# A decoder block on one core: the first row tile's scores by one matmul of 256 columns per component, an issue order written out for the passage into the up projection, and one set of transposes held

## The chip, the cores and the metric

The kernel runs on one core of a Trainium2 chip, in one launch. The metric is the device time of an execution in microseconds. Three runs of the kernel before took 675.96, 676.29 and 678.52 us; the median is 676.29.

The engines are named as in the profile: PE is TensorE's matmul, PEld its weight load, DVE is VectorE, ACT is ScalarE, POOL is GpSimd and SP is SyncE, which here only starts DMAs. Each engine works through its own instructions in a fixed order, so an instruction that waits holds back all that stand behind it on its engine.

## What is computed

One layer on 512 tokens of width 1024, all in float32:

```
h = rmsnorm(x, norm_attn_g)
q, k, v, u_pool, u_gate = split(h @ w_in)
for each head (8) and each block of 128 query rows:
    s = (rope(q) * 64**-0.5) @ rope(k).T          # two components of 64 per head
    p = softmax(where(key <= query, s, -inf))
    o = (p[0] - lam * p[1]) @ v
a = rmsnorm(o, subln_g) * (1 - lam_init)
p = causal mean over 2/4/8/16 tokens of u_pool, minus u_pool, @ w_pool, * pool_scale
x = x + (sigmoid(g_A) * a + sigmoid(g_P) * p) @ w_out
x = x + square(relu(rmsnorm(x, norm_mlp_g) @ w_up)) @ w_down
return rmsnorm(x, final_norm_g)
```

## The kernel before

**Precision.** A float32 operand is kept as two parts: `hi`, a copy rounded to the matmul's format (fp32r), and `lo`, the rest. A product is three matmuls: hi by hi, hi by lo and lo by hi. For a weight, ACT makes `hi` (line 112) and DVE the rest (line 113), or a DMA of POOL's that adds.

**The stages.** Up to some 78 us the values of all heads and the rotation tables are made. Then come the eight heads. `qk(h)` projects a head's queries and keys (`proj`, `mm3`, lines 131 to 135: eight k blocks of 512 columns, three matmuls each) and splits them. For scores the parts of one component are stacked in the 128 partitions: `qs` holds the queries' high part in one half and the rest in the other, `ks` and `kz` the matching keys, with zeros in one half of `kz`, so that a score is the sum of two matmuls with the same stationary operand (lines 395 and 396). `attn(h)` takes the query rows in four tiles of 128; tile i has (i + 1) * 128 keys. For each of two components DVE adds the mask and takes the row's extreme (397), ACT makes the exponentials (401), DVE joins the components (406), TensorE transposes blocks of 128 (410), ACT and DVE split the transposed weights (412, 413); last, twelve matmuls with the values make the head's output (418). Score tiles rotate over two PSUM banks (`sbk`), the transposed ones over two others, projections and pooled products over three (`acc`).

Between the heads stand the fillers: per group g of four, `pool(g)` and four gates, each a projection of its own. The multiplication of a gate by the row scale (474) frees its bank.

**The passage.** After the heads comes `w_out` in two halves of 512 columns. The first half accumulates all four row tiles in four banks (`po0`), the second (`po1`) row tile by row tile. `x1_add` adds the residual on DVE (588) and squares on ACT (562); after the second half, `row_scale` and line 624 make the tile's normalized row `h2`, TensorE transposes it in eight blocks (630) into two banks, and ACT and DVE take from these banks the forms in which the up projection wants it. The bank pairs alternate between even and odd tiles, so row tile 2 needs the banks of row tile 0.

The MLP multiplies its blocks of 2 x 2 with seven products in place of eight: A11, A12, A22 are plain blocks of h2 (tiles `gab`), S1 to S4 sums and differences (tiles `gss`, made in `forms_h2`, lines 597 to 604). A form of the first 256 tokens rests on row tiles 0 and 1, A22 and S1 on tiles 2 and 3, and S2, S3 and S4 on all four. For each quarter q of the hidden width, `up(q)` runs the products in the order A11, A12, S1, S2, S3, A22, S4 (q = 0), each in four groups (i, p): eight matmuls with the weights' high part (760, 762) and four with the low part (765), all of 256 columns. `keep` copies a product out of PSUM on ACT, `join` adds one to it on DVE (781). Weights named `wh_ub` and `wl_ub` are plain blocks of `w_up`, `wh_ut` and `wl_ut` sums of blocks. `down(q)` follows.

**What sets the order.** A planner orders each engine's instructions with its own estimate of when they are ready. The kernel adds edges of order to it by `after(later, earlier)`, as here:

```python
if q == 0 and form == A11 and i + p == 2 and k == 0:
    after(m, state["h2T"])
...
if form == A22:
    state["m4"] = m
elif form == S4:
    after(first[-1], state["m4"])
```

The first holds the low-part matmuls of A11's last group behind the last transpose of row tile 3; the second holds the first matmul of S4, and that one alone, behind A22. Between two instructions of one engine such an edge is an order and no wait.

Of the kernel before, what the change touches and what calls it, by code (L numbers as in the profile page):

```python
# [15 lines left out]
ALU = mybir.AluOpType  # L16
# [35 lines left out]
def block_kernel(ctx, tc, xT, x_tok, gains, pos, consts, w_in, w_v, w_pool, w_out, w_up, w_dn, out):  # L52
# [74 lines left out]
    def mm3(acc, hi, lo, rh, rl):  # L127

        for k in range(NK):
            c = slice(k * P, (k + 1) * P)  # L130
            T.matmul(acc, lhsT=hi[:, c], rhs=rh[:, k, :], start=k == 0, stop=False)  # L131
            T.matmul(acc, lhsT=hi[:, c], rhs=rl[k], start=False, stop=False)  # L132
        for k in range(NK):
            c = slice(k * P, (k + 1) * P)
            T.matmul(acc, lhsT=lo[:, c], rhs=rh[:, k, :], start=False, stop=k == NK - 1)  # L135
# [229 lines left out]
    kzs = [cf.tile([P, 2, S], F32R, name=f"kz{i}") for i in range(2)]  # L365
    for kz in kzs:
        G.memset(f(kz)[hi_, 0, :], 0.0)
        G.memset(f(kz)[lo_, 1, :], 0.0)

    def qk(h):  # L370
        qs = tp.tile([P, 2, S], F32R, tag="qs", name=f"qs{h}", bufs=2)
        ks = tp.tile([P, 2, S], F32R, tag="ks", name=f"ks{h}", bufs=2)
        kz = kzs[h % 2]
# [10 lines left out]
        return qs, ks, kz  # L384

    def attn(h, qs, ks, kz):
        wt = wt_all
        for i in range(NT):
# [3 lines left out]
            st = tmp("st", f"st{h}_{i}", (P, 6), bufs=3)  # L392
            for c in range(2):
                s_ = sbk(f"s{h}_{i}_{c}")
                T.matmul(s_[:, :N], lhsT=qs[:, c, qsl], rhs=ks[:, c, :N], start=True, stop=False)
                T.matmul(s_[:, :N], lhsT=qs[:, c, qsl], rhs=kz[:, c, :N], start=False, stop=True)  # L396
                V.tensor_tensor_reduce(  # L397
                    out=pr[:, c, :N], in0=s_[:, :N], in1=mask[:, S - N :], scale=-0.125, scalar=-NEG,
# [10 lines left out]
            for j in range(i + 1):  # L409
                T.transpose(out=t_[:, j * P : j * P + P], in_=pr[:, 0, j * P : j * P + P], identity=ident)  # L410
# [149 lines left out]
    def square(t, n, junk):  # L560

        A.activation(out=junk, in_=x1[:, t, n * 512 : n * 512 + 512], func=AF.Square, accum_out=st[:, t, n : n + 1])
# [16 lines left out]
    def mm_rows(a_, t, k, w, start, stop):  # L579
        hi, lo = w  # L580
        sl, tsl = slice((k % 2) * 512, (k % 2) * 512 + 512), slice(t * P, t * P + P)
        T.matmul(a_, lhsT=mh[:, k, tsl], rhs=hi[:, sl], start=start, stop=False)
        T.matmul(a_, lhsT=mh[:, k, tsl], rhs=lo[:, sl], start=False, stop=False)
        T.matmul(a_, lhsT=ml[:, k, tsl], rhs=hi[:, sl], start=False, stop=stop)

    def x1_add(t, n, a_):
        xs = x1[:, t, n * 512 : n * 512 + 512]
        V.tensor_tensor(out=xs, in0=a_, in1=xs, op=ALU.add)
        square(t, n, R[t][:, 0:2, :].rearrange("p a t -> p (a t)"))
# [22 lines left out]
    for t in range(NT):  # L612
        nc.sync.dma_start(out=x1[:, t, :], in_=x_tok[t])
    for t in range(NT):
        x1_add(t, 0, po[t])
        row_early(t, 0)
    g2b, _ = gain(R[4].rearrange("p b c -> p (b c)"), 0)
    ws = [get_w(w_out[1, kk], f"o1_{kk}", V) for kk in range(4)]
    for t in range(NT):
        a_ = bank(4 + t, f"po1_{t}")  # L620
        for k in range(NK):
            mm_rows(a_, t, k, ws[k // 2], k == 0, k == NK - 1)
# [3 lines left out]
        for b in range(2):  # L626
            pt = bank((t % 2) * 2 + b, f"h2T{t}_{b}")
            for j in range(4):
                k = 4 * b + j
                state["h2T"] = T.transpose(out=pt[:, j * P : j * P + P], in_=h2[:, t % 2, k * P : k * P + P], identity=ident)  # L630
# [115 lines left out]
    def up(q):  # L746
# [3 lines left out]
        def product(form, name, onto=None):  # L750
# [3 lines left out]
            for i in range(2):  # L754
                hi, lo = w[i]
                for p in range(2):
                    a_ = pa[i][:, p * HS : p * HS + HS]
                    for k in range(4):
                        c = slice((p * 4 + k) * P, (p * 4 + k) * P + P)
                        m = T.matmul(a_, lhsT=hi[:, c], rhs=rh[:, k, :], start=p + k == 0 and onto is None, stop=False, skip_group_check=True)  # L760
                        first[-1] = first[-1] or m
                        T.matmul(a_, lhsT=hi[:, c], rhs=rl[:, k, :], start=False, stop=False, skip_group_check=True)  # L762
                    for k in range(4):
                        c = slice((p * 4 + k) * P, (p * 4 + k) * P + P)
                        m = T.matmul(a_, lhsT=lo[:, c], rhs=rh[:, k, :], start=False, stop=k == 3, skip_group_check=True)  # L765
# [28 lines left out]
        def first_block():  # L794
            join(product(A12, "m2"), R[0])
# [198 lines left out]
```

## Time and profile before

| | us |
|---|---|
| median of three runs | 676.29 |
| the profiled execution | 675.88 |
| its span, from first to last instruction | 674.1 |
| PE busy in the span | 664.5 |
| PEld busy | 579.4 |
| DVE busy | 526.4 |
| ACT busy | 461.9 |
| POOL busy | 112.0 |
| TensorE's granted clock, share of full speed | 0.997 |

The profile is that of one execution. A row of a timeline gives the start, the time taken, the engine, the line, the operation, what it writes and reads, the shape and how many were merged; in brackets stands the idle time of the engine ahead of it and what ended that. A matmul's time contains its way through the array, so it overlaps the next one: what a matmul costs a full stream is the distance from its start to the next start. A row of groups gives busy time and mean nanoseconds of one, and behind the bar the idle time before. A row of waits gives who waited for whom, the time in all, how often, and the longest.

### The profile page before, as it was taken

The numbers are of one execution on the slowest core, as the hardware profiler recorded it, in microseconds if no ns is written. First come the engines' busy times: TensorE is split into PE (matmuls) and PEld (weight loads), VectorE is DVE, ScalarE is ACT, GpSimd is POOL, SyncE is SP. The second block draws the span as 40 slices with busy tenths as digits, with TensorE's granted clock in tenths as the row PEclk, the third lists the DMA queues.
The fourth block names the chain that finished last, engine by engine and source line by source line (L and its number), as shares of the span: only waits on it lengthen the run. The fifth ranks groups of instructions, "written<-read, shape, count | busy, mean of one in ns | idle before, by whom it ended". The sixth has DMA issues, their size and how long they took to land.

```text
span 674.1 us, 9988 instructions
## 1 busy us (share of the span) xinstructions
PE 664.5 (99%) x3686; PEld 579.4 (86%) x3686; DVE 526.4 (78%) x882; ACT 461.9 (69%) x741; POOL 112.0 (17%) x130
## 2 busy tenths in 40 slices
PE   9999999999999999999999999999999999999995
PEld 7888888888888888888889988899889998899884
DVE  5955977799979986965478989657994599747995
ACT  7465577978887698883477976367743696356974
POOL 2001110142133212520202020202103021210120
PEclk9999999999999999999999999999999999999998
DMA  8516464435254364574964688775959579494863
GB/s 304 174 60 182 124 150 127 101 95 124 94 133 122 98 159 95 128 197 172 314 186 84 198 176 231 159 204 138 237 187 192 194 155 261 123 215 129 215 125 124
DMA packets 32880, 109.34 MB, mean 162 GB/s; under 512 B 4032, under 2 KB 4928, under 8 KB 32832
## 3 DMA queue, kind: packets, MB, share of 16 engines
q0 software_dynamic: 10656, 38.80, 32.1%
q1 hardware_dynamic: 21744, 69.38, 28.8%
q8 instruction: 29, 0.48, 0.3%
q10 hardware_dynamic: 432, 0.52, 0.2%
q14 instruction: 19, 0.16, 0.1%
HBM read 106.59 MB, written 2.10 MB: 161 GB/s over the span
## 4 chain that ended last, share of the span: by engine, by line
PE 89%; DMA 5%; issue 3%; ACT 2%; DVE 1%; SPq 0%; POOLq 0%
PE dm L839 8%; PE dm L841 7%; PE dm L842 7%; PE um L760 7%; PE um L765 7%; PE um L762 7%; DMA wga_uNone<-w_up 4%; PE v L235 2%; PE o L418 2%; PE ga L132 2%; PE ga L131 2%; PE k L132 2%; PE gp L135 2%; PE gp L132 2%; PE k L131 2%
## 5 line engine op out<-in xcount | busy, mean ns | idle before, releaser
L841 PE MATMUL dm<-wh_dt,z 128*128 128x512 f32 (+1 forms) x128 | 49.5, 387 | 0.0
L842 PE MATMUL dm<-wl_dt,z 128*128 128x512 f32 (+1 forms) x128 | 49.4, 386 | 0.0
L839 PE MATMUL dm<-wh_dt,z 128*128 128x512 f32 (+1 forms) x128 | 49.0, 387 | 0.0
L760 PE MATMUL um<-gss,wh_ut 128*128 128x256 f32 x192 | 48.1, 284 | 0.1
L762 PE MATMUL um<-gss,wh_ut 128*128 128x256 f32 x192 | 48.1, 283 | 0.0
L401 ACT ACTIVATE p<-p,st 128x128 f32<-128x128 f32 (+3 forms) x64 | 35.7, 558 | 14.1 <-DVE st L397 13.8
L857 DVE TENSOR_TENSOR x<-x,dm 128x512 f32<-128x512 f32 x48 | 32.6, 683 | 15.2 <-PE dm L842 15.0
L112 ACT CAST wh_ut<-wga_uNone 128x1024 fp32r<-128x1024 f32 x24 | 24.9, 1052 | 27.5 <-PE dm L841 19.5
L671 POOL DMA_DIRECT2D wga_dNone<-w_dn x16 | 14.2, 885 | 150.9 <-DVE wl_dt L113 150.9
L112 ACT CAST wh_ub<-wr_u 128x1024 fp32r<-128x1024 f32 x24 | 25.1, 1048 | 20.0 <-PE um L762 11.0
L113 DVE TENSOR_TENSOR wl_ut<-wga_uNone,wh_ut 128x1024 fp32r<-128x1024 f32 x24 | 29.0, 1223 | 11.4 <-ACT wh_ut L112 10.2
L842 PE MATMUL dm<-wl_db,z 128*128 128x512 f32 x96 | 37.2, 389 | 0.0
L841 PE MATMUL dm<-wh_db,z 128*128 128x512 f32 x96 | 37.2, 389 | 0.0
L760 PEld LDWEIGHTS um<-gss,wh_ut 128*128 128x128 f32 x192 | 36.8, 192 | 0.3 <-ACT rawz L777 0.3
L762 PEld LDWEIGHTS um<-gss,wh_ut 128*128 128x128 f32 x192 | 36.9, 192 | 0.0
L839 PE MATMUL dm<-wh_db,z 128*128 128x512 f32 x96 | 35.8, 390 | 0.0
L671 POOL DMA_DIRECT2D wga_uNone<-w_up x18 | 15.6, 865 | 121.6 <-DVE wl_ut L113 87.5
L113 DVE TENSOR_TENSOR wl_ub<-wr_u,wh_ub 128x1024 fp32r<-128x1024 f32 x24 | 29.1, 1220 | 8.1 <-ACT wh_ub L112 8.1
L112 ACT CAST wh_dt<-wga_dNone 128x1024 fp32r<-128x1024 f32 x24 | 24.9, 1049 | 14.6 <-issue 5.0
L736 DVE TENSOR_TENSOR z<-rawz,z 128x1024 fp32r<-128x1024 f32 x28 | 33.7, 1221 | 0.5 <-ACT z L733 0.5
L397 DVE CUSTOM_DVE_ANT_0 p<-s,mask 128x128 f32<-128x128 f32 (+3 forms) x64 | 30.3, 484 | 3.6 <-PE s L396 3.5
L113 DVE TENSOR_TENSOR wl_dt<-wga_dNone,wh_dt 128x1024 fp32r<-128x1024 f32 x24 | 29.1, 1221 | 4.5 <-ACT wh_dt L112 4.5
(324 smaller groups left out, 2206.4 us busy)
## 6 DMA issues: line engine op xcount, KB each, us to landing
wr_u<-w_up SPq DMA_DIRECT2D x24, 512.0 KB, 5.3
wr_d<-w_dn SPq DMA_DIRECT2D x24, 512.0 KB, 4.0
wga_uNone<-w_up POOLq DMA_DIRECT2D x18, 512.0 KB, 6.8
wga_dNone<-w_dn POOLq DMA_DIRECT2D x16, 512.0 KB, 5.5
wr_k<-w_in SPq DMA_DIRECT2D x8, 512.0 KB, 3.3
wr_ga<-w_in SPq DMA_DIRECT2D x8, 512.0 KB, 3.3
wr_gp<-w_in SPq DMA_DIRECT2D x8, 512.0 KB, 3.8
wl_ga<-w_in POOLq DMA_DIRECT2D x8, 512.0 KB, 5.5
```

Of the source, the lines that this page charges most:

```text
L112: ins = A.copy(out=hi[:, sl], in_=raw[:, sl])
L113: (eng or G).tensor_tensor(out=lo[:, sl], in0=raw[:, sl], in1=f(hi)[:, sl], op=ALU.subtract)
L132: T.matmul(acc, lhsT=hi[:, c], rhs=rl[k], start=False, stop=False)
L401: A.activation(out=pr[:, c, :N], in_=pr[:, c, :N], func=AF.Exp, scale=-1.0, bias=st[:, c : c + 1], accum_out=st[:, 2 + c : 3 + c])
L736: V.tensor_tensor(out=z[:, 1], in0=r, in1=f(z[:, 0]), op=ALU.subtract)
L760: m = T.matmul(a_, lhsT=hi[:, c], rhs=rh[:, k, :], start=p + k == 0 and onto is None, stop=False, skip_group_check=True)
L762: T.matmul(a_, lhsT=hi[:, c], rhs=rl[:, k, :], start=False, stop=False, skip_group_check=True)
L765: m = T.matmul(a_, lhsT=lo[:, c], rhs=rh[:, k, :], start=False, stop=k == 3, skip_group_check=True)
L839: m = T.matmul(a_, lhsT=zh, rhs=hi[:, sl], start=p == 0 and start, stop=False, skip_group_check=True)
L841: T.matmul(a_, lhsT=zl, rhs=hi[:, sl], start=False, stop=False, skip_group_check=True)
L842: end = T.matmul(a_, lhsT=zh, rhs=lo[:, sl], start=False, stop=p == 3, skip_group_check=True)
L857: V.tensor_tensor(out=xs, in0=xs, in1=pa[a], op=(ALU.add, ALU.subtract)[n])
```

## The change

1. **Scores.** The two pieces of the keys, `ks` and `kz`, become halves of one tile `kk` of their own, two of which alternate between the heads. For the first row tile one matmul per component multiplies the queries with the first 128 columns of both pieces at once: 256 columns, whose halves lie side by side in one bank for both components. DVE adds the first half and the diagonal mask (a new operation of 128 x 256), and then the second half in the operation that already added the mask. Row tiles 1 to 3 are as before.
2. **The passage.** The four squares of the first half of `w_out` stand behind the last cast of its second half (ACT). The rows of row tiles 2 and 3 stand behind those of the tile before. The transposes of row tile 0 stand behind row tile 1's matmuls, those of tile 1 behind tile 2's, those of tile 2 behind A11's second group, those of tile 3 behind its fourth (PE). In `up(0)` each group of a product stands behind the group before it, the low-part matmuls of A12's third group stand behind the last transpose, and the two joins of A12 stand behind the low part of S2 (DVE).
3. **Transposes.** The first of the three transposes of head 6, row tile 2, stands behind the sixth matmul of the last pool projection (u3).

All edges are between instructions of one engine. The diff, cut to its core:

```diff
@@ mm3
-            T.matmul(acc, lhsT=hi[:, c], rhs=rl[k], start=False, stop=False)
+            m = T.matmul(acc, lhsT=hi[:, c], rhs=rl[k], start=False, stop=False)
+            if k == 2:
+                state["mm"] = m
@@ qk
-    kzs = [cf.tile([P, 2, S], F32R, name=f"kz{i}") for i in range(2)]
+    kks = [cf.tile([P, 2, 2, S], F32R, name=f"kk{i}") for i in range(2)]
...
-        ks = tp.tile([P, 2, S], F32R, tag="ks", name=f"ks{h}", bufs=2)
-        kz = kzs[h % 2]
+        ks, kz = (kks[h % 2][:, i] for i in range(2))
@@ attn
+            if i == 0:
+                both = sbk(f"s{h}_0").rearrange("p (c k n) -> p c k n", c=2, k=2)
+                for c in range(2):
+                    T.matmul(both[:, c], lhsT=qs[:, c, qsl], rhs=kk[:, :, c, :P], start=c == 0, stop=True, skip_group_check=True)
+                diag = mask[:, S - P :].rearrange("p (o n) -> p o n", o=1).to_broadcast([P, 2, P])
+                V.tensor_tensor(out=pr, in0=both[:, :, 0], in1=diag, op=ALU.add)
             for c in range(2):
-                s_ = sbk(f"s{h}_{i}_{c}")
-                T.matmul(s_[:, :N], lhsT=qs[:, c, qsl], rhs=ks[:, c, :N], start=True, stop=False)
-                T.matmul(s_[:, :N], lhsT=qs[:, c, qsl], rhs=kz[:, c, :N], start=False, stop=True)
+                if i:
+                    s_ = sbk(f"s{h}_{i}_{c}")
+                    T.matmul(s_[:, :N], lhsT=qs[:, c, qsl], rhs=ks[:, c, :N], start=True, stop=False)
+                    T.matmul(s_[:, :N], lhsT=qs[:, c, qsl], rhs=kz[:, c, :N], start=False, stop=True)
                 V.tensor_tensor_reduce(
-                    out=pr[:, c, :N], in0=s_[:, :N], in1=mask[:, S - N :], scale=-0.125, scalar=-NEG,
+                    out=pr[:, c, :N], in0=s_[:, :N] if i else both[:, c, 1], in1=mask[:, S - N :] if i else pr[:, c],
+                    scale=-0.125, scalar=-NEG,
...
-                T.transpose(out=t_[:, j * P : j * P + P], in_=pr[:, 0, j * P : j * P + P], identity=ident)
+                turn = T.transpose(out=t_[:, j * P : j * P + P], in_=pr[:, 0, j * P : j * P + P], identity=ident)
+                if j == 0:
+                    state["t", h, i] = turn
@@ pool
+        if g == 3:
+            after(state["t", H - 2, 2], state["mm"])
@@ w_out, second half
-        x1_add(t, 0, po[t])
+        sq0.append(x1_add(t, 0, po[t]))
...
-    ws = [get_w(w_out[1, kk], f"o1_{kk}", V) for kk in range(4)]
+    ws = []
+    for kk in range(4):
+        raw, hi, lo = load_w(w_out[1, kk], f"o1_{kk}")
+        cast = split_w(raw, hi, lo, eng=V)
+        ws.append((hi, lo))
+    for ins in sq0:
+        after(ins, cast)
...
-            mm_rows(a_, t, k, ws[k // 2], k == 0, k == NK - 1)
+            m, end = mm_rows(a_, t, k, ws[k // 2], k == 0, k == NK - 1)
+            if t > 1 and k == 0:
+                after(m, state["po"])
+        if 0 < t < 3:
+            for b in range(2):
+                after(state["h2T", t - 1, b], end)
+        state["po"] = end
...
+                if j == 1:
+                    state["h2T", t, b] = state["h2T"]
@@ up(q), product
-                        if q == 0 and form == A11 and i + p == 2 and k == 0:
+                        if q == 0 and form == A12 and (i, p, k) == (1, 0, 0):
                             after(m, state["h2T"])
+                    if q == 0:
+                        if (form, i, p) == (A11, 0, 1):
+                            for b in range(2):
+                                after(state["h2T", 2, b], m)
+                        elif (form, i, p) == (A11, 1, 1):
+                            for b in range(2):
+                                after(state["h2T", 3, b], m)
+                        if form != A11 or i + p:
+                            after(begin, state["um"])
+                        state["um"] = m
@@ join
-        def join(pa, r):
+        def join(pa, r, hold=None):
             for a_, r_ in zip(bank_view(pa), halves(r)):
-                V.tensor_tensor(out=r_, in0=a_, in1=r_, op=ALU.add)
+                ins = V.tensor_tensor(out=r_, in0=a_, in1=r_, op=ALU.add)
+                if hold:
+                    after(ins, hold)
...
-            join(product(A12, "m2"), R[0])
+            join(product(A12, "m2"), R[0], None if q else state[S2])
```

More of the change, by code (lines that the diff above doesn't have):

```diff
@@ L363, in block_kernel @@
     lo_, hi_ = slice(0, 64), slice(64, 128)
-    kzs = [cf.tile([P, 2, S], F32R, name=f"kz{i}") for i in range(2)]
-    for kz in kzs:
-        G.memset(f(kz)[hi_, 0, :], 0.0)
-        G.memset(f(kz)[lo_, 1, :], 0.0)
+    kks = [cf.tile([P, 2, 2, S], F32R, name=f"kk{i}") for i in range(2)]
+    for kk in kks:
+        G.memset(f(kk)[hi_, 1, 0, :], 0.0)
+        G.memset(f(kk)[lo_, 1, 1, :], 0.0)
     def qk(h):
         qs = tp.tile([P, 2, S], F32R, tag="qs", name=f"qs{h}", bufs=2)
-        ks = tp.tile([P, 2, S], F32R, tag="ks", name=f"ks{h}", bufs=2)
-        kz = kzs[h % 2]
+        ks, kz = (kks[h % 2][:, i] for i in range(2))
         q = rope(proj(h, f"q{h}", V) if h else q0, f"q{h}")
@@ L383, in qk, with attn @@
             V.tensor_tensor(out=ks[own, c, :], in0=k[own], in1=f(kz)[own, c, :], op=ALU.subtract)
-        return qs, ks, kz
-    def attn(h, qs, ks, kz):
+        return qs, kks[h % 2]
+    def attn(h, qs, kk):
+        ks, kz = (kk[:, i] for i in range(2))
         wt = wt_all
@@ L560, in square @@
     def square(t, n, junk):
-        A.activation(out=junk, in_=x1[:, t, n * 512 : n * 512 + 512], func=AF.Square, accum_out=st[:, t, n : n + 1])
+        return A.activation(out=junk, in_=x1[:, t, n * 512 : n * 512 + 512], func=AF.Square, accum_out=st[:, t, n : n + 1])
     def row_early(t, n):
@@ L581, in mm_rows @@
         sl, tsl = slice((k % 2) * 512, (k % 2) * 512 + 512), slice(t * P, t * P + P)
-        T.matmul(a_, lhsT=mh[:, k, tsl], rhs=hi[:, sl], start=start, stop=False)
+        m = T.matmul(a_, lhsT=mh[:, k, tsl], rhs=hi[:, sl], start=start, stop=False)
         T.matmul(a_, lhsT=mh[:, k, tsl], rhs=lo[:, sl], start=False, stop=False)
-        T.matmul(a_, lhsT=ml[:, k, tsl], rhs=hi[:, sl], start=False, stop=stop)
+        return m, T.matmul(a_, lhsT=ml[:, k, tsl], rhs=hi[:, sl], start=False, stop=stop)
     def x1_add(t, n, a_):
@@ L588, in x1_add @@
         V.tensor_tensor(out=xs, in0=a_, in1=xs, op=ALU.add)
-        square(t, n, R[t][:, 0:2, :].rearrange("p a t -> p (a t)"))
+        return square(t, n, R[t][:, 0:2, :].rearrange("p a t -> p (a t)"))
     def forms_h2(forms, x):
@@ L613, in block_kernel @@
         nc.sync.dma_start(out=x1[:, t, :], in_=x_tok[t])
+    sq0 = []
     for t in range(NT):
-        x1_add(t, 0, po[t])
+        sq0.append(x1_add(t, 0, po[t]))
         row_early(t, 0)
     g2b, _ = gain(R[4].rearrange("p b c -> p (b c)"), 0)
-    ws = [get_w(w_out[1, kk], f"o1_{kk}", V) for kk in range(4)]
+    ws = []
[5 more added lines that the diff above has]
+        after(ins, cast)
     for t in range(NT):
@@ L756, in product @@
                 for p in range(2):
+                    begin = None
                     a_ = pa[i][:, p * HS : p * HS + HS]
@@ L761, in product @@
                         first[-1] = first[-1] or m
+                        begin = begin or m
                         T.matmul(a_, lhsT=hi[:, c], rhs=rl[:, k, :], start=False, stop=False, skip_group_check=True)
```

## The prediction

> **What bounds the kernel now.** I read the page first, then the busy time by stretch, then every wait of TensorE, and then the order of its matmuls in time where a wait stands. From the page:
>
> ```profile
> span 674.1 us, 9988 instructions
> PE 664.5 (99%) x3686; PEld 579.4 (86%) x3686; DVE 526.4 (78%) x882; ACT 461.9 (69%) x741; POOL 112.0 (17%) x130
> PE 89%; DMA 5%; issue 3%; ACT 2%; DVE 1%; SPq 0%; POOLq 0%
> ```
>
> TensorE is busy 99% of the span, and the chain that ended last runs through it for 89%. Stretch by stretch (length, busy PE, PEld, DVE, ACT, POOL, then clock, DMA share and GB/s):
>
> ```profile
> 133.00:157.00 24.00, 24.00 (x120) 20.20 (x119) 22.40 (x55) 20.35 (x43) 8.57 (x10) 1.00 0.43 102
> 157.00:187.00 30.00, 30.00 (x147) 25.10 (x147) 27.19 (x57) 23.54 (x42) 6.16 (x6) 1.00 0.40 103
> 349.00:363.00 14.00, 13.39 (x109) 12.89 (x110) 12.57 (x20) 11.03 (x22) 1.72 (x2) 1.00 0.35 95
> 363.00:388.00 25.00, 24.73 (x201) 24.21 (x201) 22.89 (x24) 21.62 (x29) 1.72 (x2) 1.00 0.68 173
> ```
>
> The heads (first two rows) leave TensorE no idle time, with VectorE at 91 to 93%. The last two rows are the passage into the up projection, and there TensorE is short of 0.61 and 0.27 us. All its waits:
>
> ```profile
> PE warm L170 <- POOL eps L161: 1.1, 1, 1.1
> PE h2T L630 <- ACT h2f L647: 0.6, 1, 0.6
> PE v L235 <- ACT wh_v L112: 0.3, 1, 0.3
> PE um L760 <- ACT gss L603: 0.2, 1, 0.2
> ```
>
> Two of the four lie in the passage; the other two are at the start, which the change leaves alone. So the end moves by what TensorE's own stream loses or gains, and the prize is small: about a tenth of a per cent for each stall. A busy row hides part of it, because a matmul's length overlaps the next one; I price by distance between starts.
>
> **Term 1, the first row tile's scores.** Now there are two matmuls of 128 columns for each of two components, four per head. One such pair, and after it a pair of 256 columns from another place:
>
> ```profile
> 105.53 0.39 PE L132 MATMUL ga<-xla,wh_ga 128*128 128x512 f32 x1
> 105.75 0.22 PE L395 MATMUL s<-ks,qs 128*128 128x128 f32 x1
> 105.81 0.27 PE L396 MATMUL s<-kz,qs 128*128 128x128 f32 x1
> 105.92 0.45 PE L131 MATMUL ga<-xh,wh_ga 128*128 128x512 f32 x1
> 106.20 0.39 PE L132 MATMUL ga<-xla,wh_ga 128*128 128x512 f32 x1
> ```
>
> ```profile
> 86.30 0.28 PE L395 MATMUL s<-ks,qs 128*128 128x256 f32 x1
> 86.41 0.28 PE L396 MATMUL s<-kz,qs 128*128 128x256 f32 x1
> 86.53 0.39 PE L131 MATMUL q<-xh,wh_q 128*128 128x512 f32 x1
> ```
>
> The pair of 128 takes 0.06 and 0.11 us, and the 512-column matmul behind it takes 0.28 (105.92 to 106.20) where the usual distance is 0.22 to 0.23 (105.53 to 105.75): 0.17 + 0.05 = 0.22 us per pair. I read that as weight loads that no longer fit under so short a matmul. Two matmuls of 256 take 0.23 together and leave no tail, 0.115 each. A head goes from two pairs (0.44) to two matmuls of 256 (0.23): 0.21 us, times 8 heads 1.7 us. Bounds: without the tails (0.17 a pair, 0.34 against 0.23) 0.9 us; a trifle over 1.7 if the short ones that stand behind transposes cost more. I take 1.7, as the rows with the tail are the same shapes. The weights loaded are still the queries; the moving operand is strided over two pieces of 128, for which this trace has no row: I price it as the 256-column rows, with the 0.9 as the lower end.
>
> [...]
>
> **Its cost on VectorE.** Each head gets one addition of 128x256 out of PSUM in front of its first row's softmax. The nearest row, and the first-row operation that it feeds:
>
> ```profile
> L413 DVE TENSOR_TENSOR wt<-t,wt 128x256 fp32r<-128x256 f32 x8 | 3.3, 415 | 1.4 <-ACT wt L412 1.4
> L397 DVE CUSTOM_DVE_ANT_0 p<-s,mask 128x128 f32<-128x128 f32 x16 | 4.3, 283 | 0.5 <-PE s L396 0.5
> ```
>
> 0.415 us times 8 is 3.3 us of VectorE work, and the first row's weights come some 0.4 us later. The cover is VectorE's idle share: 1.6 us of 24 and 2.8 of 30 in the stretches above, against 0.4 added to each. TensorE meanwhile has projections to run, so I price it at 0.1 us, with 3.3 us (no cover at all) as the other end. The score banks still alternate over the two, with seven tiles a head instead of eight; the keys' pieces only change their tile.
>
> **Term 2, the passage.** The two waits in the stream:
>
> ```profile
> 348.88 0.87 PE L760 MATMUL um<-gab,wh_ub 128*128 128x256 f32 x3
> 350.36 0.66 PE L630 MATMUL h2T<-ident,h 128*128 128x128 f32 x4 [0.61 <-ACT h2f L647]
> 350.89 0.39 PE L762 MATMUL um<-gab,wh_ub 128*128 128x256 f32 x1
> ...
> 377.35 0.64 PE L765 MATMUL um<-gss,wl_ut 128*128 128x256 f32 x4
> 378.16 0.38 PE L760 MATMUL um<-gss,wh_ub 128*128 128x256 f32 x1 [0.17 <-ACT gss L603]
> 378.64 0.39 PE L760 MATMUL um<-gss,wh_ut 128*128 128x256 f32 x1
> ```
>
> In the first, the transposes of row tile 2 stand inside A11's first group and wait for the bank that tile 0's copy (L647) still holds. The idle time is 0.61; to it comes the overlap of the matmul ahead (0.38 long by the row at 378.16, next start due 0.12 later): 0.61 + 0.38 - 0.12 = 0.87 us. In the second, the four at 377.35 are due to give way 0.48 later, at 377.83; the matmul comes at 378.16 (0.33 late) and its successor at 378.64 instead of 378.28 (0.36 late): 0.69 us. It reads a plain weight block (wh_ub) against a summed form of h2 (gss), which only S4 does: a lone matmul of S4, far ahead of its product, waiting for its cast. Both go by the new order: tile 0's transposes stand right behind tile 1's rows, tile 2's behind half of A11, and every product's group behind the one before. Upper end 0.87 + 0.69 = 1.56 us.
>
> What is late next, since nothing can be pulled forward any more:
>
> ```profile
> 350.75 0.68 DVE L588 TENSOR_TENSOR x<-po,x 128x512 f32<-128x512 f32 x1
> 355.00 1.28 DVE L624 SCALAR_TENSOR_TENSOR h<-x,st,rawz 128x1024 f32<-128x1024 f32 x1
> 366.65 0.69 DVE L604 TENSOR_TENSOR gss<-hw,gss 128x512 fp32r<-128x512 f32 x1
> 367.25 1.22 DVE L599 TENSOR_TENSOR hw<-h2f,hw 128x1024 f32<-128x1024 f32 x1
> 372.33 1.23 DVE L604 TENSOR_TENSOR gss<-hw,gss 128x1024 fp32r<-128x1024 f32 x1
> 374.95 0.28 PE L760 MATMUL um<-gss,wh_ut 128*128 128x256 f32 x1
> ```
>
> Row tile 3: from its residual addition (350.75) to its normalized row (356.28) pass 5.5 us. The new order wants its transposes behind A11: 348.9 + 48 x 0.12 + 8 x 0.11 (tile 2's transposes, 0.53 for four by the rows at 350.36 at the worst) = 355.5 to 355.7. If VectorE is as busy with evictions as now, TensorE waits 0.6 to 0.8; if the earlier transposes have cleared them, the row is ready from 354.5, and nothing waits. S3: its low half is ready at 373.56, its product starts at 374.95 and needs that half one matmul later, 1.5 us of slack, and TensorE now arrives up to 1.56 earlier. The two joins of A12 (0.68 each, as L588) are put behind S2's low half on VectorE, that is right in front of S3's subtraction (367.25), up to 1.4 us later for S3. Against this, they leave the queue ahead of S2's half. Bounds for the term: 1.56 less both (0.8 + 1.4) = -0.6, to 1.56; I take 1.3, nearer the upper end because the joins free as much time ahead as they take behind.
>
> **At nothing.** The four squares held behind w_out's last cast are on ScalarE, and so are both; their row sums are read only with the second halves, some 7 us later by this stream:
>
> ```profile
> 328.16 1.03 ACT L112 CAST wh_o<-wr_o 128x1024 fp32r<-128x1024 f32 x1
> 337.94 0.30 ACT L572 ACTIVATE st<-st 128x1 f32<-128x1 f32 x1
> ```
>
> The cast can gain at most the two squares ahead of it; if the cover were gone, the squares would delay the first row by one cast, 1.03 us. No edge of the change joins two engines, so none adds a semaphore; none adds a DMA.
>
> **Term 3, the held transposes.** They now fill the time in which projection u3 waits for its bank, which the multiplication of the gate releases:
>
> ```profile
> 263.76 0.49 PE L410 MATMUL t<-ident,p 128*128 128x128 f32 x3
> 264.01 0.31 PE L395 MATMUL s<-ks,qs 128*128 128x128 f32 x1
> 264.38 0.27 PE L396 MATMUL s<-kz,qs 128*128 128x128 f32 x1
> 264.71 0.50 PE L131 MATMUL u<-xh,wh_u 128*128 128x512 f32 x1
> ...
> 263.96 0.69 DVE L474 TENSOR_TENSOR g<-gp,rb 128x512 f32<-128x512 f32 x1 [0.73 <-PE gp L135]
> ```
>
> From 264.38 a short matmul gives way 0.11 later, so u3 loses 264.71 - 264.49 = 0.22 us. Held behind u3's sixth matmul, the transposes (0.25, 263.76 to 264.01) leave this gap, and the short scores shrink by 0.2: the loss would grow by up to 0.45, unless other matmuls (the pool's six at L485 to L489 follow u3's first) come ahead. Bounds: 0.22 gained to 0.45 lost. I take 0: the rows do not tell which.
>
> **The sum.** 1.7 - 0.1 + 1.3 + 0 = 2.9 us. The profiled span of 674.1 becomes 671.2; that execution took 675.88 (1.78 around the span) and the median of the runs is 676.29, 0.41 above it. So 671.2 + 1.78 + 0.41 = **673.4 us**, 0.43% less. Behind the passage nothing takes it back: from 388 us on TensorE's matmuls stand back to back and the list has no wait of theirs.
>
> **The rivals.** (a) *New waits replace the old ones in the passage*: row tile 3 (0.8) and S3 (up to 1.4) use up 1.56, so that only the scores are left: 676.29 - 1.6 = 674.7; with the lower bound of the term, 675.3. For it: slacks of 1 us. Against: tile 3's delay now comes from evictions that would start earlier. (b) *The scores give nothing*: the tails are made up elsewhere, or the strided operand costs double; 676.29 - 1.3 = 675.0. Against: the tail is in the rows. [...] (c) *Slower: VectorE becomes the bound in the heads.* It is at 93% in the densest stretch; the added 0.415 per head lies ahead of first-row softmax, and if its idle time is all forced waiting, each head's matmuls wait for it, 3.3 us in all, the scores' gain is lost in that waiting, and the passage at its lower bound adds 0.6: 676.29 + 3.9 = 680.2; with the passage's 1.3 gained, 678.3. It decides from where the additions and waits of VectorE exceed a head's matmul time, about 1.6 us more in the densest stretch. Against: four times the added time is idle there. (d) *The order does not come out as written*, because other parts shift in the planner and both stalls reappear elsewhere: as (a).
>
> **Chances.** Forecast 0.70, with its own range 672.2 to 675.0; (a) and (d) 0.14, (b) 0.06, (c) 0.10. About 0.5% (3.4 us) is what a measurement of this kernel can tell from no change: 672.9 and 679.7. The forecast lies 0.5 above the lower one, and its upper bounds (1.7 + 1.56 + 0.22 = 3.5, and the first runs' scatter of 0.3 below the median) reach beyond, so 0.31 is faster; of (c) half passes the upper, 0.05 slower; 0.64 the same. The range runs from 671.7 (3.5, the scatter, and 0.8 for matmuls of the heads that the planner sets anew and that this trace can't price) to 677.3, which takes in (a), (b), the same 0.8 the other way and part of (c).
>
> **What would show it.** In the profile after: 16 matmuls of 256 columns more and 32 of 128 fewer in the scores, the 512-column one behind at 0.23; no wait of h2T for L647 and none of um for L603; VectorE about 3.3 us busier; PE's stream from 388 us on the same length. Wrong would be: a new wait at row tile 3's transposes or S3's first matmuls, a wait over 0.5 us ahead of u3, or idle TensorE in the heads.

## The result and the profile after

The changed kernel took 680.70 us (median of six runs, 678.36 to 681.96), the kernel before 676.07 in the same session (675.46 to 678.52). The ratio is 1.0056, 95% interval 1.0038 to 1.0074: slower by 0.56%, where 0.43% less was forecast. The profiled execution took 681.39 us.

The page of the kernel after: span, busy time of each engine, and the chain that ended last by engine.

```profile
span 679.6 us, 9962 instructions
PE 667.5 (98%) x3670; PEld 580.9 (85%) x3670; DVE 529.4 (78%) x890; ACT 458.5 (67%) x741; POOL 111.3 (16%) x130
PE 90%; DVE 4%; ACT 2%; issue 1%; POOL 1%; DMA 1%; POOLq 0%; DVEq 0%; ACTq 0%
```

Sixteen matmuls fewer, as the prediction counted, and yet PE is busy 3.0 us longer; VectorE's share of the chain has risen from 1% to 4%. TensorE's waits in the kernel after; left out are the one at the start, 1.1 us as before, and one of 0.2 us:

```profile
PE dm L883 <- ACT rawz L829: 1.9, 1, 1.9
PE s L405 <- DVE st L407: 1.5, 1, 1.5
```

The two waits in the passage that the prediction priced (h2T, and um for gss) are gone. In their place stand one in head 7 and one right behind the passage. To see what each stretch gained or lost I take the starts of the same matmuls in both kernels, at marks up to which both have issued the same work (one exception is named below). TensorE's timeline before, and with it the join of VectorE that will be needed below:

```profile
62.71 0.39 PE L131 MATMUL k<-xh,wh_k 128*128 128x512 f32 x1
...
97.90 0.39 PE L131 MATMUL gp<-xh,wh_gp 128*128 128x512 f32 x1
...
241.23 0.39 PE L131 MATMUL q<-xh,wh_q 128*128 128x512 f32 x1
...
299.70 0.39 PE L582 MATMUL po<-wh_o,vh 128*128 128x512 f32 x1
...
381.62 0.28 PE L760 MATMUL um<-gab,wh_ut 128*128 128x256 f32 x1
...
384.50 0.28 PE L762 MATMUL um<-gss,wh_ub 128*128 128x256 f32 x1
...
384.89 0.69 DVE L781 TENSOR_TENSOR rawz<-um,rawz 128x512 f32<-128x512 f32 x1
...
666.66 0.28 PE L842 MATMUL dm4b<-wl_dt,z 128*128 128x256 f32 x1
```

The same places in the timeline after, with the two waits:

```profile
63.18 0.39 PE L131 MATMUL k<-xh,wh_k 128*128 128x512 f32 x1
...
98.16 0.39 PE L131 MATMUL gp<-xh,wh_gp 128*128 128x512 f32 x1
...
123.02 0.39 PE L399 MATMUL s<-kk,qs 128*128 128x256 f32 x2
123.25 0.40 PE L132 MATMUL q<-xla,wh_q 128*128 128x512 f32 x1
...
241.48 0.39 PE L131 MATMUL q<-xh,wh_q 128*128 128x512 f32 x1
...
263.93 0.39 PE L399 MATMUL s<-kk,qs 128*128 128x256 f32 x1
265.84 0.39 PE L405 MATMUL s<-kk,qs 128*128 128x256 f32 x1 [1.52 <-DVE st L407]
...
303.08 0.39 PE L597 MATMUL po<-wh_o,vh 128*128 128x512 f32 x1
...
383.21 0.28 PE L791 MATMUL um<-gab,wh_ut 128*128 128x256 f32 x1
...
385.61 0.64 PE L797 MATMUL um<-gab,wl_ut 128*128 128x256 f32 x4
388.19 0.49 PE L883 MATMUL dm<-wh_db,z 128*128 128x512 f32 x1 [1.94 <-ACT rawz L829]
...
672.17 0.28 PE L886 MATMUL dm4b<-wl_dt,z 128*128 128x256 f32 x1
```

| stretch | before | after | difference |
|---|---|---|---|
| up to the keys of head 0 (62.71; 63.18), not touched by the change | 62.71 | 63.18 | +0.47 |
| heads 0 to 5, up to the queries of head 7 (241.23; 241.48) | 178.52 | 178.30 | -0.22 |
| the rest of the heads, to w_out (299.70; 303.08) | 58.47 | 61.60 | **+3.13** |
| the passage, to A22 (381.62; 383.21) | 81.92 | 80.13 | -1.79 |
| A22 to the last matmul (666.66; 672.17) | 285.04 | 288.96 | **+3.92** |
| sum | | | +5.51 |

The exception is one matmul of S4 (0.12 us): before it stands ahead of A22, after behind it. So the passage itself gained 1.7 us, and the stretch behind A22 lost 3.8. The waits explain half of the two losses: in head 7 265.84 - 263.93 - 0.12 = 1.8 us are lost, behind A22 388.19 - 385.61 - 4 x 0.12 = 2.1. The rest is in the clock. Two stretches of the kernel after (length, busy PE, PEld, DVE, ACT, POOL, then TensorE's granted clock, DMA share, GB/s):

```profile
266.60:269.90 3.30, 3.30 (x8) 2.54 (x9) 1.68 (x10) 3.27 (x6) 0.89 (x1) 0.50 0.89 199
...
389.50:392.80 3.30, 3.30 (x14) 2.91 (x13) 1.89 (x2) 0.93 (x2) 0.86 (x1) 0.50 0.44 140
```

Soon after each pause TensorE works at half clock for some 3.4 us (266.57 to 269.98 by the clock's record in the first, 389.45 to 392.86 in the second), which loses 1.7 us more. The first row tiles of heads 6 and 7 gain 0.4 at the price that head 0 shows (0.21, below), so the row of the heads comes to 1.8 + 1.7 - 0.4 = 3.1 and the stretch behind A22 to 2.1 + 1.7 = 3.8: both losses are accounted for. Between its start and its last matmul the trace before has no such stretch, and two of them keep PE busy 3.4 us longer, more than the 3.0 found. The granted clock of the six executions goes the same way, one stretch lowering it by 0.0025 (1.7 of 680 us): 0.997 in the one of 678.36 us, 0.994 in those of 679.95 and 680.01, 0.992 in those of 681.39 to 681.96.

### The profile page after: what moved, and what is told of

Same layout as the page of the kernel before. It is cut to its first block, busy times and chain, and to the rows that moved or that the text cites. A ratio compares the mean times of both kernels' runs of the same rounds, so it can differ in the third digit from the quotient of the medians.

```text
span 679.6 us, 9962 instructions
## 1 busy us (share of the span) xinstructions
PE 667.5 (98%) x3670; PEld 580.9 (85%) x3670; DVE 529.4 (78%) x890; ACT 458.5 (67%) x741; POOL 111.3 (16%) x130
## 4 chain that ended last, share of the span: by engine, by line
PE 90%; DVE 4%; ACT 2%; issue 1%; POOL 1%; DMA 1%; POOLq 0%; DVEq 0%; ACTq 0%
PE dm L883 8%; PE um L794 8%; PE dm L885 8%; PE um L791 7%; PE dm L886 7%; PE um L797 7%; PE v L237 2%; PE v L238 2%; PE gp L132 2%; PE gp L131 2%; PE po L598 2%; PE v L239 2%; PE po L599 2%; PE po L597 2%; PE gp L137 2%; PE ga L131 2%
## 5 line engine op out<-in xcount | busy, mean ns | idle before, releaser
L763 ACT CAST z<-rawz 128x1024 fp32r<-128x1024 f32 x28 | 28.5, 1047 | 6.5 <-DVE rawz L772 4.0
```

## The experiments

After the result I had this theory. *Head 7*: a head now uses seven score banks, not eight, and has one more VectorE operation; so VectorE's queue comes out in an order in which a late operation stands ahead of the one that frees TensorE's bank. *A22*: its second half needs a bank that VectorE's second join must read; before, the stray groups of S4 stood between the halves and covered that, and the new rule, every group behind the one before, forbids it. The rivals are named with each run. Unless another is named, the edits are made to the changed kernel. Medians of the kernel before beside the runs were 676.1 to 676.7 us.

**Each half alone.** *Scores alone* is the kernel before with item 1 of the change, *passage alone* with item 2.

> The kernel before with the scores' edit alone (no order written for the passage, no transposes held). Theory: the wait in head 7 (TensorE idle 1.5 us at the second row tile's scores in the profile after) comes from the scores' edit, the wait of down's first product (1.9 us idle) from the order of the passage. Then this kernel has the first wait, longer because head 6's transposes stand ahead of it and need the same VectorE result, none at down's first product, and the passage's old ones; gain of 1.1 us ahead of it, loss of 2 to 2.5 us by the wait and 1.7 us by a half clock behind it where that comes: 676.0 to 679.5 us. Rival: the wait comes from the passage's edges through the planner; then it's absent here and the time is about 674.5 us.

Measured: 678.05 us, ratio 1.0037 (1.0024 to 1.0050). Its waits of TensorE:

```profile
PE t L419 <- DVE p L415: 0.9, 1, 0.9
PE h2T L641 <- ACT h2f L658: 0.7, 1, 0.7
PE um L771 <- ACT gss L614: 0.7, 1, 0.7
```

> The kernel before with the order of the passage alone (scores as before, no transposes held). Theory: 1.8 us gained up to A22, then the wait of down's first product (2.1 us), with 1.7 us by a half clock where that comes: 676.1 to 678.1 us, no wait in head 7. Rival: the wait at down's first product needs the scores' edit too; then it's absent here and the time is 674.3 us.

Measured: 676.96 us, ratio 1.0016 (1.0005 to 1.0028). Its largest wait, and from its timeline the start of A22 and the last matmul:

```profile
PE dm L870 <- ACT rawz L816: 1.5, 1, 1.5
```

```profile
379.68 0.28 PE L778 MATMUL um<-gab,wh_ut 128*128 128x256 f32 x1
...
666.96 0.28 PE L873 MATMUL dm4b<-wl_dt,z 128*128 128x256 f32 x1
```

The stall of head 7 comes from the scores, the one behind A22 from the passage: each half brings its own, and each alone costs more than it gains. Of the loss of the scores alone some 0.9 us lies in the passage, though, where the two old waits last longer (0.7 and 0.7 us) and one of 0.4 us joins them. With the passage alone A22 starts 1.9 us earlier than before (379.68 against 381.62), and from there to the end pass 287.28 us, 2.24 more. The excesses (1.8 and 0.7 us) add up to 2.5 of the changed kernel's 4.6 us: alone, neither of the two profiled executions had half clock.

**The queue in head 7: five runs.** First, head 7's scores of row tile 1 held behind u3's sixth matmul as well, so that u3 stands first:

```diff
+                    m = T.matmul(s_[:, :N], lhsT=qs[:, c, qsl], rhs=ks[:, c, :N], start=True, stop=False)
+                    state["s", h, i, c] = m
...
         if g == 3:
             after(state["t", H - 2, 2], state["mm"])
+            after(state["s", H - 1, 1, 0], state["mm"])
```

> The changed kernel, with the first scores of head 7's row tile 1, which wait in it, also held behind u3's sixth matmul. If the bank of these scores alone is late, the stream runs on into u3 and 1.9 us are gained, and the half clock of 1.7 us behind the wait goes where it came: 677 to 679 us. If VectorE's queue as a whole is late there (it stands 1.8 us behind ScalarE's result for head 6), then u3, whose bank is freed by the same queue, waits in its place and nothing is gained: 680 to 681 us.

Measured: 682.03 us, ratio 1.0082 (1.0070 to 1.0094).

```profile
PE u L131 <- DVE g L491: 2.1, 1, 2.1
```

The wait moved to the next matmul that needs VectorE, and grew: the queue is late, and not one bank alone. Why it is late, VectorE's timeline of the changed kernel shows, with two rows of the engines beside it:

```profile
258.05 1.11 POOL L440 TENSOR_TENSOR sqo<-o 128x512 f32<-128x512 f32 x1
...
258.12 1.60 DVE L356 TENSOR_TENSOR q1k<-q1k,swk 128x512 f32<-128x512 f32 x1
259.85 0.54 DVE L407 CUSTOM_DVE_ANT_0 p<-s,mask 128x384 f32<-128x384 f32 x1
...
263.90 0.62 ACT L416 ACTIVATE p<-p,st 128x384 f32<-128x384 f32 x1
...
264.55 0.62 DVE L417 SCALAR_TENSOR_TENSOR p<-p,st 128x384 f32<-128x384 f32 x1 [1.78 <-ACT p L416]
265.09 0.69 DVE L407 CUSTOM_DVE_ANT_0 p<-s,mask 128x512 f32<-128x512 f32 x1
...
265.70 0.69 DVE L489 TENSOR_TENSOR g<-gp,rb 128x512 f32<-128x512 f32 x1
```

Row tile 2 of head 6 (384 columns) gets its second mask only at 259.85, behind the key's rotation (L356). From there it passes through the queues of both engines: its exponential starts at 261.04 behind casts of the keys on ScalarE, its reciprocal at 262.36 behind a subtraction for the keys on VectorE, and L416, whose factor is ready at 262.78, at 263.90 behind an exponential of row tile 3 and another cast; so 1.1 us of what follows is ScalarE's order. L416 ends at 264.52, VectorE stands 1.78 us ahead of the joining of the components (L417), and behind that wait the mask of row tile 3 (265.09), which frees the score bank, and the gate (265.70), which frees u3's. Second, the same kernel without the added VectorE operation. The first piece of the first row tile's scores is then left out, and the score banks still go by seven.

```diff
-                diag = mask[:, S - P :].rearrange("p (o n) -> p o n", o=1).to_broadcast([P, 2, P])
-                V.tensor_tensor(out=pr, in0=both[:, :, 0], in1=diag, op=ALU.add)
...
-                    ... in1=mask[:, S - N :] if i else pr[:, c],
+                    ... in1=mask[:, S - N :],
```

> The changed kernel without VectorE's added operation: the first piece of the first row tile's scores is computed but not added, so one part of these scores is left out; seven score banks a head, as in the changed kernel. Theory (the bank rotation of seven makes pairs straddle row tiles, and this sets up the 1.85 us wait in head 7): a wait of 1.5 us or more on VectorE's freeing of a score bank or a gate's bank is still there in head 7, the wait of down's first product too, and the median is 679 to 681. Rival (VectorE's eight additions, 0.4 us each, are what makes it late): the wait in head 7 is below 0.5 us, the end of u3 comes 3 to 4 us earlier, and the median is 676.5 to 678.5.

Measured: 675.83 us, ratio 0.9993 (0.9981 to 1.0006). VectorE's timeline:

```profile
256.24 0.55 DVE L405 CUSTOM_DVE_ANT_0 p<-s,mask 128x384 f32<-128x384 f32 x1
...
257.52 0.68 DVE L352 TENSOR_TENSOR q1k<-k,tab 128x512 f32<-128x512 f32 x1
...
260.47 0.62 DVE L415 SCALAR_TENSOR_TENSOR p<-p,st 128x384 f32<-128x384 f32 x1
```

The mask now stands ahead of the rotation, and L415 waits for nothing. In head 7 a wait of 0.5 us is left, on ACT's cast of the keys; behind A22 it is 1.2 us in this execution, and the median lies 0.7 us below the range of either side. So seven banks a head are not enough for the stall, and that part of my theory falls; without the addition, in the order that then comes out, it does not appear. Third, one score bank skipped ahead of each first row tile, so that the pairs stand as before:

```diff
             if i == 0:
+                sbk.n += 1
                 both = sbk(f"s{h}_0").rearrange("p (c k n) -> p c k n", c=2, k=2)
```

> The changed kernel with the rotation of the score banks advanced by one more at each first row tile, so that a head takes eight steps again and the two components of a row tile are always issued as a pair. Theory: with seven steps the pairs straddle row tiles in every second head, head 6's third and fourth tiles are late, and that makes the wait in head 7; then it's gone here, 1.9 us and the half clock's 1.7 us with it, 677 to 678.5 us, and the wait of down's first product stays. Rival: the added VectorE operation or ScalarE's order makes it late; then a wait of 1.5 us or more stays ahead of u3, 680 to 681 us.

Measured: 677.28 us, ratio 1.0020 (1.0009 to 1.0031). The waits that bear on it:

```profile
PE dm L884 <- ACT rawz L830: 2.2, 1, 2.2
...
PE q L131 <- DVE g L490: 0.9, 1, 0.9
```

The wait of 1.5 us in head 7 is down to 0.2, as forecast, but a projection waits 0.9 us for VectorE at 186 us, in another head. In head 6 the second mask of row tile 2 stands behind the rotation of head 7's keys here too (at 257.97); but that step is short, 0.69 us, and starts 0.22 us ahead of GpSimd's operation:

```profile
257.36 0.69 DVE L356 TENSOR_TENSOR q1k<-q1k,swk 128x512 f32<-128x512 f32 x1
...
257.58 1.36 POOL L441 TENSOR_TENSOR sqo<-o 128x512 f32<-128x512 f32 x1
```

Fourth, to tell the bank from the order: the skip in head 6 alone leaves TensorE's order in the heads as it was, and only lets the two banks change places from there on. Here and in the run after it S4's groups also stand between A22's halves, as described below.

```diff
+                if h == H - 2:
+                    sbk.n += 1
```

> The same with the skip ahead of head 6 alone: TensorE's order in the heads stays that of the changed kernel, only the two banks change places from head 6 on. If it is the bank that matters: the 1.5 to 1.9 us wait in head 7 goes. If it is VectorE's queue and the order of the scores that matter (my theory by now): the wait stays, 1.5 us or more, median 676.2 to 678.2 as with S4's groups put back alone.

Measured: 676.36 us, ratio 1.0001 (0.9987 to 1.0015).

```profile
PE s L407 <- DVE st L409: 1.5, 1, 1.5
```

The same wait, to a tenth: the bank is ruled out, and the order and the timing of the queue are left. With the skip in heads 6 and 7 (`if h >= H - 2`):

> S4's groups between A22's halves, and one score bank skipped ahead of the first row tile in heads 6 and 7 alone, so that only there the two components of a row tile again take the two banks in turn. If the skip in the earlier heads is what cost the version with both mends its 0.9 us wait at 186 us (1.1 us lost), and the skip in heads 6 and 7 what cured the wait ahead of u3: no wait over 0.5 us in the heads, median 673.9 to 674.8. If the wait at 186 us has another cause, or the one ahead of u3 needs the skip in all heads: a wait of 0.9 us or more in one of the two places, median 675.2 to 676.5.

Measured: 676.54 us, ratio 0.9997 (0.9983 to 1.0010), with a wait of 1.7 us ahead of head 7's first scores. The wait at 186 us is gone, but the one in head 7 isn't cured: it is the second case of the forecast. A stall of some 1 to 2 us is passed from place to place by each edit that reorders the queues, and which edit sends it where I could not foresee.

One rival none of these runs tested. In all eight traces in which VectorE stands 1.78 or 1.79 us ahead of that joining, the key's last rotation step takes 1.58 to 1.60 us, beside GpSimd's multiplication; in the eight others it takes 0.68 or 0.69, and VectorE waits there 0.22 us or not at all. The step stands in the queue ahead of the mask, so by an estimate from these rows 0.9 of the 1.8 us lost in head 7 comes from it. The two small delays of the heads look alike: ahead of them a joining of the components takes 1.78 us (at 153.98) and 1.13 (at 225.70) beside GpSimd's operations (153.49 to 155.21; 225.17 to 226.68). That the scores' edit brings the stall, and that it is gone without the addition, is shown; how much of it is the order itself and how much the meeting with GpSimd stays open.

**Without holding the transposes** (item 3 undone):

```diff
-        if g == 3:
-            after(state["t", H - 2, 2], state["mm"])
```

> The changed kernel without the held transposes. Theory: head 6's transposes then stand ahead of head 7's second row tile and wait for the same VectorE queue, so that the wait ahead of u3 only changes its name: 1.2 to 1.5 us idle at the transposes and some tenths behind; within 0.5 us of the changed kernel when neither or both have the half clock, 679 to 681 us. Rival: holding them makes the wait; without it 2 to 3 us faster, 677 to 678.5 us.

Measured: 678.59 us, ratio 1.0041 (1.0026 to 1.0056).

```profile
PE t L421 <- DVE p L417: 0.9, 1, 0.9
```

Unheld, the transposes wait for the same late L417, 0.9 us of idle time in place of 1.5. Holding them gave TensorE nothing to do in the gap: the next in its order waits behind that operation too. The median lies between the two forecasts: 0.4 us under the one, 0.1 over the other.

**A22: three runs.** First, the down projection's first product held behind A22, since its matmul was the one that waited:

```diff
+                if q == 0 and form == A11:
+                    after(m, state["m4"])
```

> The changed kernel, with down's first product held behind A22's last matmul. Theory: the planner drew eight of its matmuls between A22's halves, where their bank is still to be emptied; held, they cost nothing: 2.1 us gained, and 1.7 us more where a half clock followed: 676.5 to 678.5 us, the wait in head 7 left. Rival: A22's second half is itself late (its weights), so that TensorE waits there in place of it: under 0.5 us gained.

Measured: 680.17 us, ratio 1.0064 (1.0050 to 1.0079). The wait, and the clock behind it:

```profile
PE um L791 <- DVE rawz L823: 3.1, 1, 3.1
```

```profile
387.10:393.80 6.70, 6.14 (x28) 6.14 (x29) 3.16 (x4) 2.72 (x4) 0.86 (x1) 0.50 0.59 141
```

The pause grew, so the place of the down projection was not at fault, and this part of my theory fell. Now A22's second half itself waits, for VectorE's join (L823). In the changed kernel that join is at

```profile
387.30 1.22 DVE L766 TENSOR_TENSOR z<-rawz,z 128x1024 fp32r<-128x1024 f32 x1
388.44 0.68 DVE L823 TENSOR_TENSOR rawz<-um,rawz 128x512 f32<-128x512 f32 x1
```

and before it was at 384.89, while TensorE had 23 matmuls of S4 to run between A22's halves (from 384.50 on). Second and third, those two groups of S4 are let in again, in the changed kernel and in the passage alone:

```diff
-                        if form != A11 or i + p:
+                        state["up", form, i, p] = begin, m
+                        if form == S4 and p == 0:
+                            after(begin, state["up", A22, i, 1][1])
+                        elif form != A11 or i + p:
                             after(begin, state["um"])
+                        if (form, i, p) == (S4, 0, 1):
+                            after(state["up", A22, 1, 0][0], m)
...
-            elif form == S4:
+            elif form == S4 and q:
                 after(first[-1], state["m4"])
```

> The changed kernel with one thing undone: S4's first two groups may stand between the halves of A22 again, so that VectorE's second join has cover. My theory (the strict order of groups took that cover away): the wait of the down projection's first product for the read of z is gone, and with it the stretch at half clock behind it; the 2.1 us (and up to 1.7 us more) come back, so the median falls from 680.7 to between 677.0 and 678.6. The wait of head 7's scores (1.85 us) is untouched and stays, with or without its half-clock stretch. Rival (the waiting only moves, because the read of z is late by itself): a new wait of 1 us or more behind A22, and the median stays at 680 to 681.

Measured: 676.49 us, ratio 1.0009 (0.9998 to 1.0020): 4.2 us less than the changed kernel, half a microsecond below the range I gave. No wait is left behind A22; the one in head 7 stays at 1.5 us.

> The passage alone (scores as before, nothing held in the heads), with one change of its order: S4's first two groups stand between A22's halves, as most of them did in the kernel before, in place of behind A22. Theory: A22's second half must wait for S3's join on VectorE (its bank), and S4's 24 matmuls (2.9 us) were the work that hid this; with them back the wait at down's first product is gone and the passage's 1.8 us stay: 674.2 to 674.8 us. Rival: the join or S4's own forms come too late all the same, because VectorE's order has changed; a wait of 0.5 to 1.5 us stays and the time is 675 to 676 us.

Measured: 675.29 us, ratio 0.9993 (0.9981 to 1.0005). A22's start, and the last matmul:

```profile
380.07 0.28 PE L778 MATMUL um<-gab,wh_ut 128*128 128x256 f32 x1
...
665.39 0.28 PE L878 MATMUL dm4b<-wl_dt,z 128*128 128x256 f32 x1
```

From A22 to the end 285.32 us: 0.28 more than before, where the passage alone lost 2.24. In both kernels the wait goes when the cover is back: the missing cover is shown as the cause. The median is half a microsecond above the range given for this case.

**Both mends together** (score banks in pairs, S4 between A22's halves), and the same without holding, and without the addition:

> The changed kernel with both mends: score banks paired, and S4's first two groups between A22's halves. If both theories hold, the scores' gain of 1.1 to 1.7 us and the passage's 1.8 us are left: 673.0 to 674.5 us, under the kernel before. If the one of the banks falls, 676 to 678 us; if the one of S4 falls, 676 to 678.5 us.

Measured: 675.36 us, ratio 0.9995 (0.9984 to 1.0006); the wait of 0.9 us at 186 us is the only one over 0.5 us behind the start. The median is 0.9 us above the range in which both gains would be left.

> Both mends and the transposes of head 6 not held: the whole change otherwise. If holding still costs once the score banks stand in pairs: 674.7 to 675.1. If it costs nothing there, as the short waits left in head 7 suggest (0.2 to 0.3 us): 675.2 to 675.6, the same as with both mends.

Measured: 675.82 us, ratio 0.9994 (0.9984 to 1.0004). Not to be told from the one before: with the banks in pairs, holding costs nothing that shows. The median is 0.2 us above the forecast for that case.

> Both mends (score banks in pairs, S4's groups between A22's halves) and without VectorE's added operation: the first piece of the first row tile's scores is left out of the sum. It prices the addition itself against the version with both mends (675.4). If the addition costs TensorE its remaining waits in the heads (0.9 us for a projection's bank, some 0.2 us more of lost starts): 673.8 to 674.4. If it lies in VectorE's idle time and the 0.9 us wait has another cause: 675.0 to 675.7.

Measured: 683.00 us, ratio 1.0103 (1.0088 to 1.0119), which neither side expected.

```profile
PE po L597 <- DMA wl_o<-w_out: 2.7, 1, 2.7
```

As a price of the addition this run is of no use: another order of ScalarE's queue made a weight's rest late for w_out (its operation on ScalarE starts at 298.38, with both mends at 294.50). It shows how large the effect of the order is: leaving an operation out cost over 7 us against the run with both mends.

No version beats the kernel before by more than the interval; the best are 0.05 to 0.07% below it.

## Why the prediction was wrong

**What bounds the kernel** was right: TensorE's stream sets the end, and the whole difference is found in it. That also holds for the gains.

**Term 1, the scores: right for one head, and mostly lost again over six.** Forecast 0.21 us a head; head 0 gained it: the difference of 0.47 at its keys (62.71; 63.18) is 0.26 at the gate behind it (97.90; 98.16). But heads 0 to 5 together gained 0.22 in place of 1.26. Two small delays of 0.2 to 0.3 us (at 156 and 226 us) took 0.5 of the rest; where the other half went stays open. The pair of 256 columns takes 0.23 us and leaves no tail (123.02 to 123.25): the strided operand has the price of the plain one. For the tail of the pair of 128 the prediction named the weight loads, and the rows of before agree: a load takes 0.19 us, and the matmul at 106.20 starts 0.04 us behind the end of its own (105.97 to 106.16), as the one at 105.53 does (105.30 to 105.49). No run changed the loads alone. Rival (b), that the scores give nothing, came near in the sum over the heads, but neither of its reasons shows.

**The addition on VectorE: priced at 0.1, and this is the first step that failed.** The operation itself takes what was forecast:

```profile
L401 DVE TENSOR_TENSOR p<-s,mask 128x256 f32<-128x256 f32 x8 | 3.3, 416 | 0.0
```

But the cover was worked out as a share of idle time over 24 and 30 us, and the loss is in one place: in head 7 VectorE stands 1.78 us while it is needed right behind, and TensorE loses 1.8. VectorE's idle time elsewhere (busy 78% of the span) was no cover here. Nor did the price take in that a shifted operation can come to stand beside one of GpSimd's, as the key's rotation step does (1.60 us there, 0.68 in the kernel before). Rival (c) had the side and the engine right, and its form wrong: not each head's matmuls wait, but one head's. That its price (678.3 to 680.2) lies near the 680.70 measured is luck: the sum is made of things it didn't contain.

**Term 2, the passage: the gain was there, 1.7 us where 1.3 was forecast and 1.56 was the upper bound.** The 0.1 above the bound stays open. Of the two named as late next, row tile 3 and S3's low half, neither made TensorE wait. Rival (a) had the kind of loss right, a new wait in place of the old, but looked for it at row tile 3 and S3.

**"Behind the passage nothing takes it back" is the second step that failed.** The lone matmul of S4 was seen ahead of its product and taken for a stray. It was the first of a row that the planner had put between A22's halves, and these hid the join that the second half needs. The prediction asked which waits the order removes, and not which waits the old order hid. For the held squares of w_out the prediction did ask what their cover was; for S4 it did not ask what S4 covered where it stood. The signs were in the profile before: rows of S4 (384.50) between rows of A22, and a join at 384.89.

**Term 3, held transposes: 0 forecast, within its bounds but for the clock.** The runs give 0.9 us of idle time unheld, 1.5 held, and the medians 678.59 and 680.70. From the queries of head 7 to the last gate the profiled executions take 53.61 us unheld (241.66 to 295.27) and 55.46 held (241.48 to 296.94). Of the 1.85 between them 1.7 are the half clock, which followed the longer pause and not the shorter; 0.15 is left for the holding itself, under the bound of 0.45.

**The clock** stood nowhere in the prediction: the trace before has no half clock between its start and its last matmul. With the 1.7 us that a stretch at half clock lost in the kernel after, a price for a stall of 2 us should have been 2 to 3.7.

The half clock alone doesn't explain the miss: the range ended at 677.3, and the fastest of the six runs took 678.36 at a granted clock of 0.997, that of the kernel before. The chance of slower was 0.05, from half of rival (c) alone; the second failed step had no rival at all.

## What to carry to other kernels

Before tightening an order by hand, list what the old order had hidden: for each matmul that seems to stray into another product, look at which bank or buffer is being freed meanwhile, and leave it there if something is. For an engine that works in order, price an added operation at the narrowest place of its queue, not against its idle share. Here TensorE's stalls of 1.8 and 2.1 us came to 3.5 and 3.8 us with the half clock behind them, and waits of up to 1.3 us had none behind them: by an estimate from these, two separate stalls of 1 us are cheaper than one of 2; no run compared them. Where an operation moves, look also at what GpSimd does at its new place: here the key's rotation step took 1.60 us beside its multiplication, 0.68 without in the kernel before.

## What was not expected of the hardware

**Half clock after pauses of 2 us.** The same pause, in the same order of TensorE in the heads, was followed by half clock in one execution and not in another. The stretch behind the 1.5 us wait in head 7, in the run with S4 between A22's halves:

```profile
269.30:272.00 2.70, 2.70 (x8) 2.14 (x7) 0.71 (x4) 2.67 (x4) 0.26 (x1) 0.50 0.85 168
```

and in the run that only shifts the banks from head 6 on:

```profile
266.00:269.00 3.00, 2.94 (x13) 2.35 (x14) 1.90 (x11) 2.97 (x6) 0.89 (x1) 1.00 0.81 205
```

The first of these executions took 679.56 us, the second 675.99; 2.1 us of that are there before the heads (the keys of head 0 at 64.92 against 62.80). In the profiles of this study the waits of up to 1.3 us had no half clock behind them, of those from 1.4 to 1.9 us some had and some not, and those of 2.1, 2.2 and 2.7 us all had one stretch (granted clock of these executions 0.991, 0.994 and 0.995), the one of 3.1 us one twice as long (0.993). The clock's record in the trace of the kernel after: full for 259.41 us, half for 3.41, full for 119.47, half for 3.41, full for 283.31; in that of the kernel before: full for 665.60 in one piece. The full stretches are 76, 35, 83 and 195 times 3.413 us long. What it is in a pause of 1.4 to 1.9 us that brings the half clock, or not, is not shown: no run moved a pause alone.

**VectorE beside GpSimd.** The key's last rotation step took 1.60 us (258.12) where the same step for the queries took 0.69 at 251.83, while GpSimd multiplied from 258.05 on (1.11 us). In the kernel before (259.45) and in the run without the addition (259.64) the step took 0.68 us, behind the end of GpSimd's multiplication and subtraction (257.11; 258.76). No run here took GpSimd's operation away, so that it is what lengthens the step is not shown.
